# Three tiles of the pooled input move to the context's tiles, with a new order of copies, masks and norms around them

## The chip, the cores and the metric

One NeuronCore of a Trainium2 chip runs the whole program in one launch. The metric is the device time of an execution in microseconds (us), from its start to its end; less is better. TensorE (PE) multiplies matrices, VectorE (DVE), ScalarE (ACT) and GpSimd (POOL) work on elements, SyncE (SP) issues all DMAs from one queue, in order. Each engine runs its instructions strictly in the order in which the program put them there, and waits at the first whose inputs or buffers are not ready.

## The reference

One layer of a hybrid trunk, fp32, 1024 latent tokens (a grid of 16 x 64) and 256 context tokens, width 1024:

```python
h = rms_norm(x) * (1 + scale) + shift                 # modulated, as is the context
q, k, v, ab, z, u, zp = split(h @ w_in)               # one projection, q..z of 8 heads x 128
o = gated_delta_rule(conv(q), conv(k), conv(v), ...)  # 8 heads, both directions, chunks; decay masked to a triangle
y1 = norm(o) * silu(z)
y2 = (box_mean(u) - u) @ pool_w * scale * silu(zp)    # 4 groups, windows 2, 4, 8, 16
out = rms_norm(x + gate * (concat(y1, y2) @ w_out))
```

The context's tokens go through the same projection (only k and v of them are needed) and give the state with which the latent scans begin.

## The kernel before

**Tiles.** The input projection is done in tiles of 128 output columns. Every fp32 operand is split into a high part, rounded to fp32r, and a low part (the rest), and a product takes three passes (high by high, low input by high weights, high input by low weights). A tile over the 1024 latent tokens (letters `h` for a head's v, k, z or q, `z` for a gate of the pooling, `u` for a pooled input) is 48 matmuls of 128x512, in two halves; a tile over the context (`c`) is 24 matmuls of 128x256; `a` makes the decays. A tile's weights come by one DMA of 512 KB (`wraw`, or `kT` for some early ones); ScalarE makes `whi`, GpSimd `wlo`.

**Order.** `SEQ` and what follows it give the order of the tiles, and `main()` walks through it. All other work is in threads (`x_sums`, `inputs`, `thread_a` and so on), which a planner, class `Flow`, weaves in between by the costs in `Engine.cost`. It runs while the program is built, so on the chip the order on each engine is fixed. In the code all engine calls go through one helper line, L364, and all DMAs through L382; operations are therefore told apart by the names of their tiles.

**The front.** After the modulation, TensorE runs `c` tiles. Each is evacuated by ScalarE (`u<-mm`, `kT<-mm` or `vT<-mm`) and then convolved on VectorE: four `scalar_tensor_tensor` of 128x256, a tanh on ScalarE and a fifth `scalar_tensor_tensor`. Beside them the latent input x, eight tiles of 128 tokens (four in each half: `B`, `ks`, `qd` are their buffers), is normalised: a sum of squares on ScalarE (`vn`), the root on GpSimd (`rstd`, two operations), the product on VectorE. `x_half` then transposes it on TensorE in 16 pieces of 128x512 (`pp<-ident,B` and so on), ScalarE modulates each into `tmp`, `W`, `XT` or `Y` in turn, `x_split` has VectorE make `hnhi` (CAST) and VectorE or GpSimd `hnlo`. Only when all 16 are split (flag `hn`) can a tile over the latent tokens start. The first such tiles are two `z` tiles, whose evacuation needs a tanh on ScalarE (`tmp<-mm`) and one operation on VectorE (`ks<-tmp,mm`).

**The heads.** Thirty-two `h` tiles with `z` tiles among them, and for every head in turn `stage_a` to the scan. `stage_d` loads a head's decays (`D<-gscr`) and has GpSimd add a triangular mask to them (`D<-D,mask`, 128x512, four for every head and four for each of two groups of context heads), before ScalarE takes the exponential.

**The tail.** After the last tile of `main()` the heads' buffers are released and `out_main` begins: `u_tiles` runs the eight `u` tiles on TensorE (evacuated by ScalarE into three buffers `ups`, in turn), `mix_all` makes the box means on VectorE (tiles `ws`, `rp`; at the end of each `dhi` on ScalarE and `dlo` on VectorE), `pool_out` multiplies each group by its weights `pw` and evacuates with a VectorE operation (`zp<-pp,psc,zp`) and a DMA to `yscr`. The output projection takes the first three token tiles together, 288 matmuls of 128x512: first those of the heads' eight k tiles (flag `heads`), then those of the pooled eight. `second_half` loads the weights for the latter once the last `dlo` is there (flag `mixed`). Five more token tiles follow.

Of the kernel before, what the change touches and what calls it, by code (L numbers as in the profile page):

```python
# [8 lines left out]
FP32 = mybir.dt.float32  # L9
FP32R = mybir.dt.float32r  # L10
I32 = mybir.dt.int32
ACTF = mybir.ActivationFunctionType
# [19 lines left out]
DRAMS = ("gscr0", "gscr1", "escr", "sscr", "yscr", "zscr", "uscr", "gate", "ds", "vs")  # L32
SEQ = "cccccccccccccczccazhhhzhhhhhhhhhhhhhhhhhhhhhhhhhhhhh"
KB = 3
# [279 lines left out]
class Engine:  # L314
# [3 lines left out]
    def cost(self, op, a, k):  # L318
# [24 lines left out]
        if op == "tensor_copy":  # L343
            return 80.0 + 3.8 * n
        if op == "memset":
            return 36.0 + 0.83 * n
# [44 lines left out]
def kernel(  # L391
# [90 lines left out]
    ident = const.tile([P, P], FP32, name="ident")  # L482
    mask = [const.tile([P, P], FP32, name=f"mask{d}") for d in range(2)]
    tri = [dl_tile([P, P], "S", 2) for d in range(2)]
# [48 lines left out]
    for d in range(2):  # L533
        pool.memset(mask[d], 0.0)
        pool.memset(tri[d], 1.0)
        s = 1 if d == 0 else -1
        pool.affine_select(out=mask[d], in_=mask[d], pattern=[[s, P]], compare_op=ALU.is_ge, fill=NEG,
                           base=0, channel_multiplier=-s)
        pool.affine_select(out=tri[d], in_=tri[d], pattern=[[s, P]], compare_op=ALU.is_ge, fill=0.0,
                           base=0, channel_multiplier=-s)  # L540
# [23 lines left out]

    def norm_root(col):
        s = rstd[:, col:col + 1]
        pool.tensor_scalar(out=s, in0=s, scalar1=1.0 / D, scalar2=EPS, op0=ALU.mult, op1=ALU.add)
        power(s, 0)
# [87 lines left out]
    CH = [2 * g + i for g in GROUPS for i in range(2)]  # L656
    NZ = tiles[:tiles.index("h")].count("z")
    kinds = dict(c=iter([t * D + h * P for h in range(H) for t in (1, 2)]),
# [54 lines left out]
    def x_sums():  # L713
        for k in range(NB):
            flow.settle(landed[k])
            yield "act" if XACT & 1 else None
            norm_sum(xs[k], k)
            norm_root(k)
            yield "dve" if XACT & 2 else None
            norm_mul(xs[k], k)  # L720
            if k % 4 == 3:
                flow.flag("xs", k // 4)

# [245 lines left out]
    def stage_d(J, part):  # L969


        t = J.PT[part] = dl_tile([P, 2, 4, P], f"D{part}", 2)
        r = J.h * (NB if J.is_x else NBC)
        for d in range(2):
            rd = r + 4 * (part ^ d)
            sync.dma_start(out=t[:, d].rearrange("p b i -> p (b i)"), in_=gscr[J.is_x][d, rd:rd + 4, :].rearrange(
                "b i -> (b i)").partition_broadcast(P))
        yield
        for d in range(2):
            pool.tensor_tensor(out=t[:, d], in0=t[:, d], in1=rep(mask[d], 4), op=ALU.add)  # L980
            if d or DY < 8:
                yield
            for b in range(4):
                act.activation(out=t[:, d, b, :], in_=t[:, d, b, :], func=ACTF.Exp,
                               bias=J.col("ngc", d, 4 * (part ^ d) + b))
                if b % DY == DY - 1:
                    yield "act" if XACT & 16 else None
        flow.flag("D", J.key, part)
# [399 lines left out]
    def x_half(hf):  # L1388
        for k in range(KT):
# [9 lines left out]
            if XACT & 4:  # L1399
# [3 lines left out]
                           scale=md[:, 0, 1, k:k + 1], bias=md[:, 0, 0, k:k + 1])  # L1403
            flow.give()
            flow.flag("h32", n)
            flow.add(x_split(hf, k, h32), [("h32", n)], True)

    def x_split(hf, k, h32):
        if XACT & 8:
            yield "dve"  # L1410
        dve.tensor_copy(hn[2 * hf][:, k, :], h32)
        yield
        e = dve if k % XD == 0 else pool
        e.tensor_tensor(out=hn[2 * hf + 1][:, k, :], in0=h32, in1=hn[2 * hf][:, k, :], op=ALU.subtract)
        flow.flag("split", hf * KT + k)
# [29 lines left out]
    def z_tile(h):  # L1445
# [3 lines left out]
        flow.flag("z", h)  # L1449

    def zp_tile(t):

        yield ("hn",)
        if t > 1:
            yield ("zp", t - 2)
        zs = dl_tile([P, L], "ks", 2)
        yield from gate_tile(hnx, zs)
        sync.dma_start(out=zscr[CH[t]], in_=zs)
        flow.flag("zp", t)

# [23 lines left out]
    def thread_a():  # L1484
# [3 lines left out]
        for k in range(-2, H):  # L1488
            yield ("k", k)
            yield ("ab", k >= 0)  # L1490
            yield ("done", k - 2)
            yield from stage_a(jobs[k])

# [6 lines left out]
    def thread_s():  # L1500
        for k in range(-2, H):
# [5 lines left out]
            else:  # L1507
                yield ("ab", True)
                if NZ:
                    yield ("zp", NZ - 1)  # L1510
                yield from stage_k(jobs[k])
# [73 lines left out]
    def main():  # L1585
        kinds = dict(c=ctx, a=iter([ab_tile()]), u=iter([u_early(n) for n in range(UP)]),
                     z=iter([(zp_tile if i < NZ else zp_late)(i) for i in range(ZP)]),
# [241 lines left out]
    def out_main():  # L1829
# [139 lines left out]
        def second_half():  # L1969
            yield ("mixed",)  # L1970
            pl_p.release()
            pools["c"] = Pool(flow, tc.alloc_tile_pool(name="outc", bufs=1, side="right", reuse_waits="tile"))
# [110 lines left out]
```

## Time and profile before

| | before |
|---|---|
| median of 3 runs | 1317.15 us (1315.63 to 1318.1) |
| the profiled execution | 1321.76 us |
| its span, first to last instruction | 1320.0 us |
| mean granted TensorE clock | 0.962 |
| busy: PE, DVE, ACT, POOL | 1212.5, 928.0, 570.8, 438.7 us |
| instructions of 128x512 projection matmuls | 3 x 768 |

The busy times are of the whole span; what an engine does in one stage is read from windows, and what it waited for from the timeline. A matmul's record is longer than its share of the engine, since matmuls overlap; their number in a window in which TensorE never waits gives the time of one.

### The profile page before, as it was taken

The page shows a single profiled execution, that of the slowest core. Times are in us where ns is not written, and L with a number is a line of the kernel's source. Part 1 is how long each engine was busy: PE and PEld are TensorE (multiplying, and loading weights), DVE is VectorE, ACT ScalarE, POOL GpSimd, SP SyncE. Part 2 cuts the span into 40 slices and gives each one's busy share as a digit, 9 for nine tenths or more (in the row PEclk, how much of TensorE's full clock was granted, in tenths as well). Part 3 has the DMA queues.
Part 4 walks back from the last instruction along what each step waited for, and adds up shares of the span by engine and source line. Part 5 has one row for each costly group of instructions (what it writes and reads, how often), then busy time and mean ns, then how long its engine had stood idle before and what let it go on. Part 6 is the DMA issues. An engine that isn't in the chain of part 4 may idle for free.

```text
span 1320.0 us, 26398 instructions
## 1 busy us (share of the span) xinstructions
PE 1212.5 (92%) x10631; PEld 977.8 (74%) x10631; DVE 928.0 (70%) x1883; ACT 570.8 (43%) x1498; POOL 438.7 (33%) x451
## 2 busy tenths in 40 slices
PE   8876699899899999999999989999999999799997
PEld 2666577677777877788778768778788777688887
DVE  4799989868886787877776867878433999724212
ACT  3466437444436547455474464643613123322110
POOL 2477433230421423314132233141215454402330
PEclk9788899899999999989999999999999899899999
DMA  9533344223121213212221131212313135565230
GB/s 329 188 99 93 86 140 125 74 57 90 37 49 48 78 42 100 58 46 80 49 83 44 41 100 41 69 63 43 103 60 109 48 104 185 199 206 157 83 112 32
DMA packets 157384, 123.73 MB, mean 94 GB/s; under 512 B 47106, under 2 KB 135115, under 8 KB 157261
## 3 DMA queue, kind: packets, MB, share of 16 engines
q1 hardware_dynamic: 157261, 122.04, 30.6%
q8 instruction: 83, 1.36, 0.4%
q14 instruction: 40, 0.33, 0.1%
HBM read 101.43 MB, written 20.60 MB: 92 GB/s over the span
## 4 chain that ended last, share of the span: by engine, by line
PE 40%; DVE 14%; ACT 6%; DMA 2%; issue 2%; POOL 2%; DVEq 0%; SPq 0%; POOLq 0%; ACTq 0%
PE mm L364 24%; PE sc L364 5%; PE o L364 4%; DVE kT L364 4%; PE pp L364 3%; PE pa L364 3%; DVE t L364 3%; DVE ws L364 3%; ACT junk L364 2%; ACT ks L364 1%; DMA D<-gscr 1%; DVE dlo L364 1%; DVE rp L364 1%; POOL wlo L364 1%; DVE zp L364 1%
## 5 line engine op out<-in xcount | busy, mean ns | idle before, releaser
L364 PE MATMUL mm<-hnhi,whi 128*128 128x512 f32 x768 | 321.0, 418 | 0.9 <-ACT whi L364 0.9
L364 PE MATMUL mm<-hnhi,wlo 128*128 128x512 f32 x768 | 316.7, 412 | 2.0 <-POOL wlo L364 2.0
L364 PE MATMUL mm<-hnlo,whi 128*128 128x512 f32 x768 | 316.9, 413 | 0.0
L364 POOL TENSOR_TENSOR wlo<-wraw,whi 128x512 fp32r<-128x512 f32 x110 | 158.0, 1442 | 337.3 <-ACT whi L364 330.5
L364 PEld LDWEIGHTS mm<-hnhi,whi 128*128 128x128 f32 x768 | 147.7, 192 | 26.8 <-issue 1.7
L364 PEld LDWEIGHTS mm<-hnhi,wlo 128*128 128x128 f32 x768 | 146.9, 191 | 26.0 <-POOL wlo L364 2.5
L364 PEld LDWEIGHTS mm<-hnlo,whi 128*128 128x128 f32 x768 | 147.6, 192 | 22.9
L364 DVE SCALAR_TENSOR_TENSOR kT<-u,cw,kT 128x512 f32<-128x512 f32 (+1 forms) x96 | 94.8, 994 | 5.3 <-ACT kT L364 1.8
L364 POOL TENSOR_TENSOR D<-D,mask 128x512 f32<-128x512 f32 x40 | 58.9, 1478 | 92.3 <-DMA D<-gscr 76.8
L364 ACT ACTIVATE y<-sc 128x256 f32<-128x256 f32 (+1 forms) x65 | 24.9, 383 | 131.3 <-PE sc L364 125.3
L364 ACT ACTIVATE u<-mm 128x512 f32<-128x512 f32 (+1 forms) x64 | 34.8, 543 | 88.3 <-PE mm L364 88.1
L364 DVE SCALAR_TENSOR_TENSOR t<-t,laneN 128x1 f32<-128x1 f32 (+4 forms) x150 | 68.0, 453 | 6.8 <-DMA laneN<-ds 2.8
L364 ACT ACTIVATE whi<-wraw 128x512 fp32r<-128x512 f32 x110 | 67.5, 633 | 1.8 <-DMA wraw<-in_w_in_dram 1.5
L364 DVE SCALAR_TENSOR_TENSOR vT<-u,cw,vT 128x512 f32<-128x512 f32 (+1 forms) x80 | 67.2, 843 | 1.5
L364 DVE TENSOR_TENSOR pw<-mm,zp 128x512 f32<-128x512 f32 (+1 forms) x12 | 8.0, 669 | 83.9 <-PE mm L364 83.9
L364 ACT ACTIVATE D<-D,ngc 128x128 f32<-128x128 f32 x160 | 53.1, 403 | 30.7 <-POOL D L364 30.7
L364 DVE SCALAR_TENSOR_TENSOR qT<-u,cw,qT 128x512 f32<-128x512 f32 (+1 forms) x80 | 63.0, 788 | 2.9 <-ACT qT L364 1.2
L364 DVE SCALAR_TENSOR_TENSOR S<-S,egl,sc 128x128 f32<-128x128 f32 x112 | 33.7, 343 | 33.4 <-PE sc L364 30.4
L364 DVE SCALAR_TENSOR_TENSOR r<-sc,neg,vn 128x128 f32<-128x128 f32 x128 | 38.7, 345 | 23.0 <-PE sc L364 22.9
L364 PEld LDWEIGHTS sc<-S,kT 128*128 128x128 f32 x256 | 36.9, 192 | 15.6 <-issue 9.1
L364 PE MATMUL mm<-D,whi 128*128 128x256 f32 x128 | 41.2, 322 | 7.3 <-DVE ks L364 4.5
L364 PE MATMUL sc<-S,kT 128*128 128x128 f32 x256 | 40.7, 282 | 7.2 <-DVE S L364 6.7
(409 smaller groups left out, 2785.5 us busy)
## 6 DMA issues: line engine op xcount, KB each, us to landing
wraw<-in_w_in_dram SPq DMA_DIRECT2D x55, 512.0 KB, 3.8
D<-gscr SPq DMA_DIRECT2D x40, 256.0 KB, 4.1
qd<-escr SPq DMA_DIRECT2D x16, 512.0 KB
kT<-in_w_in_dram SPq DMA_DIRECT2D x9, 512.0 KB, 4.0
whnhi<-in_w_mod_dram SPq DMA_DIRECT2D x8, 512.0 KB, 3.5
whnlo<-in_w_mod_dram SPq DMA_DIRECT2D x8, 512.0 KB, 9.5
D<-in_w_mod_dram SPq DMA_DIRECT2D x8, 512.0 KB, 4.9
yscr<-zs SPq DMA_DIRECT2D x8, 512.0 KB, 2.8
```

What stands on the lines that cost most here:

```text
L364: return f(*a, **k)
```

## The change

- `SEQ`: instead of 14 `c`, `z`, 2 `c`, `a`, `z` ahead of the first head there are 11 `c`, `u`, 2 `c`, `u`, 2 `c`, `u`, `a`, `c`, `z`. The number of tiles is the same; one `z` more comes behind the last head's tiles (six instead of five).
- The three early `u` tiles are evacuated by two ScalarE copies each into a `ks` buffer and stored to `uscr`; after the heads they are read back into `ups`. Five `u` tiles stay in the tail.
- `x_half`: ScalarE makes `hnhi` right after the modulated piece, and `x_split` is left with the subtraction for `hnlo`. `thread_a` also waits until the first half's pieces are made.
- `stage_d`: one `affine_select` in place of the addition of a mask; the two mask tiles and their making are gone.
- `x_sums`: four sums of squares, one root for four columns, four products, instead of one after the other.
- `second_half` also waits for the last group's pooling weights.

```diff
-SEQ = "cccccccccccccczccazhhhzhhhhhhhhhhhhhhhhhhhhhhhhhhhhh"
+SEQ = "cccccccccccuccuccuaczhhhzhhhhhhhhhhhhhhhhhhhhhhhhhhhhh"
...
-    def norm_root(col):
-        s = rstd[:, col:col + 1]
+    def norm_root(col, n=1):
+        s = rstd[:, col:col + n]
...
     def x_sums():
-        for k in range(NB):
-            flow.settle(landed[k])
-            yield "act" if XACT & 1 else None
-            norm_sum(xs[k], k)
-            norm_root(k)
-            yield "dve" if XACT & 2 else None
-            norm_mul(xs[k], k)
-            if k % 4 == 3:
-                flow.flag("xs", k // 4)
+        for hf in range(2):
+            ks = range(4 * hf, 4 * hf + 4)
+            for k in ks:
+                flow.settle(landed[k])
+                yield "act"
+                norm_sum(xs[k], k)
+            yield
+            norm_root(4 * hf, 4)
+            for k in ks:
+                yield "dve"
+                norm_mul(xs[k], k)
+            flow.flag("xs", hf)
...
         for d in range(2):
-            pool.tensor_tensor(out=t[:, d], in0=t[:, d], in1=rep(mask[d], 4), op=ALU.add)
+            s = 1 - 2 * d
+            pool.affine_select(out=t[:, d], in_=t[:, d], pattern=[[0, 4], [s, P]], compare_op=ALU.is_ge, fill=NEG,
+                               base=0, channel_multiplier=-s)
...
             flow.give()
+            act.activation(out=hn[2 * hf][:, k, :], in_=h32, func=ACTF.Copy)
             flow.flag("h32", n)
             flow.add(x_split(hf, k, h32), [("h32", n)], True)
+        flow.flag("xt", hf)
 
     def x_split(hf, k, h32):
-        if XACT & 8:
-            yield "dve"
-        dve.tensor_copy(hn[2 * hf][:, k, :], h32)
-        yield
+        yield "pool" if k % XD else "dve"
         e = dve if k % XD == 0 else pool
...
+    def ahead(dst, tile):
+
+        i = aheads[0]
+        aheads[0] += 1
+        yield ("hn",)
+        if i > 1:
+            yield ("ahead", i - 2)
+        s = dl_tile([P, L], "ks", 2)
+        yield from tile(s)
+        sync.dma_start(out=dst, in_=s)
+        flow.flag("ahead", i)
...
+    def u_tile(n):
+        def tile(s):
+            def evac(ps, t0):
+                act.activation(out=s[:, t0:t0 + 512], in_=ps, func=ACTF.Copy)
+
+            yield from gemm_tile(hnx, L, evac)
+
+        yield from ahead(uscr[n], tile)
...
-                if NZ:
-                    yield ("zp", NZ - 1)
+                if NZ + NUA:
+                    yield ("ahead", NZ + NUA - 1)
...
         def second_half():
             yield ("mixed",)
+            yield ("pw", GROUPS[-1])
```

**Where instructions move.** On TensorE, ahead of the first tile that reads `hn`, before: the transposes of x's second half (from `ks` and `qd`) stand among the matmuls of `c` tiles (`mm<-D` and `mm<-zs`).

```order
L364 MATMUL mm<-D_230,wlo 128x256
L364 MATMUL pp<-ident,ks 128x128 x2
L364 MATMUL pp<-ident,qd 128x128 x2
L364 MATMUL mm<-D_230,whi 128x256
L364 MATMUL mm<-zs,whi 128x256
L364 MATMUL mm<-D_230,wlo 128x256
L364 MATMUL mm<-D_229,whi 128x256
```

The same place of the changed kernel, from the last matmul of the eleventh `c` tile to the first of the first `u` tile, with the middle left out:

```order
L366 MATMUL mm<-D_220,wlo 128x256
L366 MATMUL pp<-ident,B 128x128 x8
L366 MATMUL pp<-ident,ks 128x128 x2
L366 MATMUL pp<-ident,qd 128x128 x2
L366 MATMUL pa<-kT 128x128 x4
...
L366 MATMUL pp<-ident,ks 128x128 x2
L366 MATMUL pp<-ident,qd 128x128 x2
L366 MATMUL pa<-ident,vT 128x128 x4
L366 MATMUL mm<-hnhi_223,whi 128x512
L366 MATMUL mm<-hnlo_224,whi 128x512
```

All eight transposes of the second half, and two of the first, now stand between the eleventh `c` tile and the first `u` tile with no tile's matmuls among them.

On ScalarE, the last pieces of x before the change:

```order
L364 ACTIVATE tmp<-pp,md 128x512
L364 ACTIVATE W<-pp,md 128x512
L364 ACTIVATE u<-mm 128x256
L364 ACTIVATE qT<-mm,cw 128x256
L364 ACTIVATE D_983<-D_983,ngc_238 128x128 x4
L364 ACTIVATE whi<-kT 128x512
L364 ACTIVATE XT<-pp,md 128x512
L364 ACTIVATE whi<-kT 128x512
L364 ACTIVATE Y<-pp,md 128x512
```

and now:

```order
L366 ACTIVATE tmp<-pp,md 128x512
L366 ACTIVATE hnhi_225<-tmp 128x512
L366 ACTIVATE W<-pp,md 128x512
L366 ACTIVATE hnhi_225<-W 128x512
L366 ACTIVATE XT<-pp,md 128x512
L366 ACTIVATE hnhi_225<-XT 128x512
L366 ACTIVATE t_1162<-B,half_of 32x128 x4
L366 ACTIVATE t_1162<-bt,half_of 128x128
L366 ACTIVATE D_1167<-D_1167,ngc_228 128x128 x2
L366 ACTIVATE Y<-pp,md 128x512
L366 ACTIVATE hnhi_225<-Y 128x512
```

Pieces and their copies stand in pairs, and the evacuations of `c` tiles that stood between them are ahead of them.

On SyncE's queue, the change from the heads to the tail, before:

```order
L382 DMA zscr<-u 128x1024
L382 DMA yscr<-zs 128x1024
L382 DMA pwr<-in_pool_w_dram 128x2x256
L382 DMA zp<-zscr 128x1024 x2
L382 DMA wraw<-in_w_in_dram 128x8x128 x4
```

and now (`zscr<-u` stores the last `z` tile):

```order
L384 DMA yscr<-zs 128x1024
L384 DMA zscr<-u 128x1024
L384 DMA ups_11395<-uscr 128x16x64
L384 DMA ups_11396<-uscr 128x16x64
L384 DMA ups_11397<-uscr 128x16x64
L384 DMA pwr<-in_pool_w_dram 128x2x256
L384 DMA zp<-zscr 128x1024 x2
```

The three loads of `ups` stand behind the store of the last `z` tile, which waits for that tile's last VectorE operation.

## Rows read from the trace of the kernel before

**Rows 1.** Windows: start:end length, busy us (x) of PE, PEld, DVE, ACT, POOL, granted clock, DMA.

```profile
46.00:134.50 88.50, 62.81 (x409) 58.12 (x408) 83.32 (x141) 53.12 (x122) 59.69 (x77) 0.85 0.32 90
134.50:193.20 58.70, 48.59 (x590) 36.70 (x591) 50.80 (x97) 23.35 (x63) 23.20 (x24) 0.91 0.36 101
...
260.00:1005.00 745.00, 708.58 (x7577) 582.23 (x7575) 538.41 (x1285) 368.46 (x1066) 210.96 (x213) 0.98 0.22 62
1016.80:1138.50 121.70, 113.28 (x480) 91.55 (x479) 116.85 (x110) 32.52 (x45) 59.42 (x34) 0.97 0.33 107
1160.00:1200.00 40.00, 40.00 (x178) 33.02 (x177) 9.95 (x12) 9.64 (x15) 9.52 (x8) 1.00 0.50 164
```

**Rows 2.** VectorE's operations by form, 46 to 134.5 us: busy us, mean ns, idle before.

```profile
L364 DVE SCALAR_TENSOR_TENSOR vT<-u,cw,vT 128x256 f32<-128x256 f32 x16 | 15.3, 956 | 0.4
L364 DVE SCALAR_TENSOR_TENSOR kT<-u,cw,kT 128x256 f32<-128x256 f32 x23 | 15.2, 659 | 2.3 <-ACT kT L364 1.8
L364 DVE CAST hnhi<-XT 128x512 fp32r<-128x512 f32 x4 | 6.2, 1554 | 0.0
L364 DVE CAST hnhi<-tmp 128x512 fp32r<-128x512 f32 x4 | 4.0, 1003 | 0.2 <-ACT tmp L364 0.2
...
L364 DVE CAST hnhi<-W 128x512 fp32r<-128x512 f32 x4 | 2.7, 683 | 0.0
...
L364 DVE CAST hnhi<-Y 128x512 fp32r<-128x512 f32 x4 | 2.6, 638 | 0.0
```

**Rows 3.** Timeline of VectorE, 680 to 701 us: start, length, operation.

```profile
683.68 11.27 DVE L364 SCALAR_TENSOR_TENSOR kT<-u,cw,kT 128x512 f32<-128x512 f32 x8
...
699.86 1.29 DVE L364 SCALAR_TENSOR_TENSOR kT<-u,kT 128x512 f32<-128x512 f32 x2
```

**Rows 4.** Timeline of GpSimd, same stretch.

```profile
685.31 1.28 POOL L364 TENSOR_TENSOR wlo<-wraw,whi 128x512 fp32r<-128x512 f32 x1 [2.59 <-ACT whi L364]
686.53 1.75 POOL L364 TENSOR_TENSOR D<-D,mask 128x512 f32<-128x512 f32 x1
```

**Rows 5.** GpSimd's operations by form, 46 to 134.5 us.

```profile
L364 POOL TENSOR_TENSOR D<-D,mask 128x512 f32<-128x512 f32 x4 | 5.9, 1482 | 0.0
...
L364 POOL TENSOR_TENSOR rstd<-rstd,expo 128x1 f32<-128x1 f32 x8 | 5.5, 684 | 0.7
```

**Rows 6.** ScalarE's operations by form, 46 to 134.5 us.

```profile
L364 ACT ACTIVATE W<-pp,md 128x512 f32<-128x512 f32 x4 | 3.1, 779 | 1.9 <-PE pp L364 1.9
```

**Rows 7.** Timeline of TensorE at the first matmul that reads hn.

```profile
134.51 0.50 PE L364 MATMUL mm<-hnhi,whi 128*128 128x512 f32 x1 [0.87 <-ACT whi L364]
```

**Rows 8.** TensorE's waits, 134 to 194 us: tile, releaser, total us, times, longest.

```profile
PE mm L364 <- DVE ks L364: 4.5, 1, 4.5
```

**Rows 9.** GpSimd's affine_select on tile t: count, ns min/median/max, first and last start.

```profile
L364 POOL TENSOR_SCALAR_AFFINE_SELECT t<-t x10: 510/510/705, 145.6 to 900.4; 128x256 f32<-128x256 f32 x10
```

**Rows 10.** TensorE's waits, 200 to 960 us.

```profile
PE pa L364 <- DVE kT L364: 12.4, 7, 3.6
```

**Rows 11.** Timeline of VectorE, the end of the heads and the pooling.

```profile
1005.31 0.69 DVE L364 SCALAR_TENSOR_TENSOR u<-tmp,mm 128x512 f32<-128x512 f32 x1 [4.44 <-ACT tmp L364]
...
1016.77 1.58 DVE L364 TENSOR_TENSOR ws<-ups 128x1120 f32<-128x1120 f32 x1 [1.36 <-ACT ups L364]
...
1136.11 0.74 DVE L364 SCALAR_TENSOR_TENSOR zp<-pp,psc,zp 128x512 f32<-128x512 f32 x1
1137.32 1.23 DVE L364 TENSOR_TENSOR dlo<-ws,dhi 128x1024 fp32r<-128x1024 f32 x1 [0.47 <-ACT dhi L364]
```

**Rows 12.** Timeline of SyncE's queue: a load of y pieces is issued.

```profile
1100.88 0.38 SPq L382 DMA_DIRECT2D wraw<-yscr  x1
```

**Rows 13.** Timeline of ScalarE: the first operation that reads what was loaded.

```profile
1106.67 1.06 ACT L364 ACTIVATE yhi<-wraw 128x1024 fp32r<-128x1024 f32 x1 [3.51 <-DMA wraw<-yscr]
```

**Rows 14.** GpSimd's operations by form, 1016.8 to 1138.5 us.

```profile
L364 POOL TENSOR_TENSOR wlo<-wraw,whi 128x512 fp32r<-128x512 f32 x12 | 24.4, 2046 | 36.3 <-ACT whi L364 36.3
```

**Rows 15.** Timeline of TensorE at the last pooled group.

```profile
1144.92 0.80 PE L364 MATMUL pp<-dhi,pw 128*128 128x512 f32 x1 [7.06 <-ACT pw L364]
```

More of the change, by code (lines that the diff above doesn't have):

```diff
@@ L344, in cost @@
             return 80.0 + 3.8 * n
+        if op == "affine_select":
+            return 80.0 + 1.7 * n
         if op == "memset":
@@ L482 @@
     ident = const.tile([P, P], FP32, name="ident")
-    mask = [const.tile([P, P], FP32, name=f"mask{d}") for d in range(2)]
     tri = [dl_tile([P, P], "S", 2) for d in range(2)]
@@ L533 @@
     for d in range(2):
-        pool.memset(mask[d], 0.0)
         pool.memset(tri[d], 1.0)
         s = 1 if d == 0 else -1
-        pool.affine_select(out=mask[d], in_=mask[d], pattern=[[s, P]], compare_op=ALU.is_ge, fill=NEG,
-                           base=0, channel_multiplier=-s)
         pool.affine_select(out=tri[d], in_=tri[d], pattern=[[s, P]], compare_op=ALU.is_ge, fill=0.0,
@@ L656 @@
     CH = [2 * g + i for g in GROUPS for i in range(2)]
-    NZ = tiles[:tiles.index("h")].count("z")
+    NZ, NUA = [tiles[:tiles.index("h")].count(c) for c in "zu"]
     kinds = dict(c=iter([t * D + h * P for h in range(H) for t in (1, 2)]),
@@ L1449, in z_tile @@
         flow.flag("z", h)
-    def zp_tile(t):
[L1453 to L1459, printed above, removed]
+    def ahead(dst, tile):
[8 more added lines that the diff above has]
+        flow.flag("ahead", i)
+    aheads = [0]
+    def zp_tile(t):
+        yield from ahead(zscr[CH[t]], lambda s: gate_tile(hnx, s))
+    def u_tile(n):
[4 more added lines that the diff above has]
+        yield from ahead(uscr[n], tile)
     def zp_late(t):
@@ L1491, in thread_a @@
             yield ("done", k - 2)
+            yield ("xt", 0)
             yield from stage_a(jobs[k])
@@ L1585, in main @@
     def main():
-        kinds = dict(c=ctx, a=iter([ab_tile()]), u=iter([u_early(n) for n in range(UP)]),
+        kinds = dict(c=ctx, a=iter([ab_tile()]), u=iter([(u_tile if n < NUA else u_early)(n) for n in range(UP)]),
                      z=iter([(zp_tile if i < NZ else zp_late)(i) for i in range(ZP)]),
```

## Prediction

> **What bounds the kernel now.** I read the windows by stage first, then for each stage the engine that never rests. TensorE is nearly full through the heads (708.6 of 745 us from 260 to 1005) and full in the output projection; what it loses, it loses at both ends [rows 1]. From 46 to 134.5 us it works 62.8 of 88.5 us, and VectorE 83.3: VectorE is the bound, and `hn`, the point at which the first tile over the latent tokens can start, came at 134.51 [rows 1, 7]. From there to 193.2, where the first head's tile starts, TensorE rests another 58.7 - 48.6 = 10.1 us, 4.5 of them because a `z` tile's evacuation stood in VectorE's queue [rows 1, 8]; the clock of 0.91 means that some 18% of the stretch ran at the lower level, which cost about 5 us. In the tail VectorE is the bound again: the pooling runs on it from 1016.77 to 1138.5 and fills 116.9 of 121.7 us, while TensorE has 113.3 us of records there and then a wait of 7 us for the last group's weights [rows 1, 11, 15]. So the tail is as long as VectorE's chain, not as TensorE's work. A tile of 48 matmuls costs 48 x 40 / 178 = 10.8 us at full clock, from the window without waits [rows 1].
>
> **VectorE is slowed by GpSimd.** The eight steps of a k convolution took 11.27 us, 1.41 each, while GpSimd ran additions and subtractions of 1.28 and 1.75 us; two steps of the same size just behind them took 0.65 each [rows 3, 4]. In the front the 256-wide steps took 0.66 and 0.96 us on average, about twice what half of 0.65 would be, and one kind of CAST took 0.64 and another 1.55 [rows 2].
>
> **Step 1, when `hn` comes.** The 16 casts leave VectorE: 6.2 + 4.0 + 2.7 + 2.6 = 15.5 us [rows 2]. GpSimd loses two-input work there: six of eight roots (0.68 each), the splits of the three `c` tiles that now come later (six of about 1.4), a part of the masks (5.9 in all) [rows 5], together some 15 of its 59.7 us. VectorE's 39 convolution steps of these two kinds hold about 17 us above half of 0.65 each, so I credit 15/59.7 of that, 4 us. Against it, VectorE's order now has two more convolutions and a few small operations of the context's stage ahead of the last split, about 4 us. That gives 134.5 - 15.5 - 4 + 4 = 119. ScalarE now has 16 copies more, at about the 0.78 of a piece or less [rows 6], and in the order the last eight pieces stand as pairs with nothing between them: they cannot start before VectorE has normalised x's second half, behind its convolutions. I take 121. The bounds are 110 (every us that GpSimd gives back is one of VectorE's) and 131 (the copies, some 10 us, come wholly behind VectorE).
>
> **Step 2, from `hn` to the first head.** Now four tiles (43.2 us), five `c` tiles (24 matmuls of half the width, 2.7 each, 13.5), the decays (32 matmuls, 7.2) and the context's own stage. That stage is what remains of the old stretch: 58.7 - 10.1 waits - 5 for the clock - 21.6 - 5.4 - 7.2 = 9.4. The `u` tiles are evacuated by ScalarE alone, so the 4.5 us wait on VectorE should go; of the old 15 us of waits and low clock I keep 6. Sum 79, so the first head starts at 200 instead of 193.2: **+7**. TensorE does two tiles (21.6 us) more by then, so 15 of them are hidden; the pauses from 46 on had room for 36.
>
> **Step 3, heads.** The order keeps four tiles to a head, so their length stays except for waits. One mask addition in each head falls into the k convolution, for whose end TensorE waited seven times, 12.4 us in all [rows 4, 10]. The trace has no select of 128x512; one of half the size took 0.51 [rows 9], so between 0.51 and 1.02 against 1.28 to 1.75. If it slows VectorE for as long as it lasts, a head gains some 0.4 us, if not at all up to 1.7; **-4**, bounds 0 and -12. The Trainium skill ("SBUF — State Buffer", SBUF: two separate sides) says that GpSimd and VectorE share a port pair that is locked for a whole instruction, by any GpSimd operation that reads SBUF against a VectorE operation with two SBUF inputs. The convolution's 1.41 against 0.65 agrees with it; by that rule the select still locks VectorE out while it runs, and this step would be nearer to -3.
>
> **Step 4, one `z` tile more behind the heads: +10.8.** It stands ahead of everything in the tail on every queue that matters: VectorE's pooling comes behind its gate, and SyncE's loads of `ups` behind its store.
>
> **Step 5, start of the pooling.** Before, it began 10.8 us after the last gate (1006.0 to 1016.77), the time of a `u` tile [rows 11]. Now it needs a read-back. The nearest row is the load of `yscr`, 5.8 us from issue to its first use [rows 12, 13]; with 5.5 this is **-5.3** (bounds -4 and -7.5).
>
> **Step 6, the pooling itself.** The same operations on VectorE. Under them stood 12 weight splits of 2.05 us on GpSimd [rows 14]; with five `u` tiles left it is eight. **-5**, bounds 0 and -8.2. The 33 us of TensorE's work that leave the tail give nothing: TensorE has five tiles (54), twelve of sixteen pool products (16) and 66 output matmuls (15) to do before the last group, 85 us, against VectorE's 5.5 + 117 + 6. It will rest some 43 us there.
>
> **Step 7, after the last `dlo`.** Before, the last group's first product came 6.4 us after `dlo`, 8.1 us after the evacuation that frees the way for its weights [rows 11, 15]. Now that evacuation stands behind the last `dlo`, but fewer loads stand ahead of the weights. From that product to the end of the first three token tiles the order has 246 matmuls instead of 237. **+2**, bounds 0 and +5. The 120 us behind them are unchanged.
>
> **Sum.** 7 - 4 + 10.8 - 5.3 - 5 + 2 = +5.5 us. The profiled execution took 1321.76 us (span 1320.0), 4.6 above the median of the runs; so 1327.3 for one like it, and 1317.15 + 5.5 = **1322.7** for the median. Costed at nothing: the mask tiles, made at the program's start while the modulation's weights are loading, at most four operations of 0.51 us on GpSimd if that cover were gone [rows 9]; the three stores of 512 KB to `uscr`, on DMA engines that are busy 0.36 of that stretch [rows 1]; the wait added to `thread_a`, behind which the context's first stage is queued, whose matmuls stand among the last transposes and have four tiles beside them (uncovered it would be part of rival B); and the wait in `second_half`, behind which only loads stand that are needed some 30 us later.
>
> **Rivals.**
> A, faster: VectorE gets the whole of what GpSimd gives back, and `hn` comes at 110. Then everything behind it is 11 us earlier: 1311 to 1312. For it: the convolution row shows nearly one us lost for each us of GpSimd. Against it: the last eight pairs on ScalarE have to follow the normalisation. It decides at an `hn` of about 115.5, where the sum is nil.
> B, a new wait: the pairs on ScalarE become the bound, `hn` at 131, hardly earlier than before. 5.5 + 10 = 15.5, so 1333. For it: no tile's matmuls stand beside the last transposes, so nothing covers them.
> C, the tail follows TensorE's work: the three tiles taken out (32.4 us) come off its end. With steps 2 to 4 that is 7 - 4 + 10.8 - 32.4, about 1299. Against it: VectorE's 117 us in 122.
> D, the select or the read-back does not give what I credit: steps 3, 5 and 6 at their poor bounds make 5.5 + 4 + 1.3 + 5, 1333; it shares its place with B.
>
> **How the numbers follow.** What a measurement can tell from no change is about 0.2%, 2.6 us. The forecast (1317 to 1329) has 0.5, A (1307 to 1316) 0.25, B with D (1329 to 1337) 0.19, C 0.06. Slower is all of B and D and three quarters of the forecast: 0.57. No change is the forecast's lower end and a little of A: 0.14. Faster is the rest: 0.29. The range goes from 1306 to 1335, which leaves out C and the ends of A and B.
>
> **What would show it.** The first matmul that reads `hn` at 121, the first head's tile at 200; the last gate about 14 us later than before; the first `ws<-ups` 5.5 us behind it; the last `dlo` 117 us after that; and TensorE resting some 40 us in the tail. The sum is wrong if `hn` comes before 115, or if VectorE is not busy through the pooling.

## The result, and the profile after

The changed kernel took 1329.76 us (median of 4 runs, 1327.1 to 1332.19) against 1317.27 us for the kernel before on the same chip (4 runs, 1315.63 to 1318.1): a ratio of 1.0096 [1.0071, 1.012], some 12.5 us slower. Slower was the forecast's sign; its 1322.7 was 7 us short, inside the range.

The two profiled executions stand closer together than the medians: their spans are 1320.0 and 1325.4 us, since the one before lies above the median of its kernel and the one after (1327.1 us) is the fastest of its own. The steps below are read from that pair and add up to +5.4 us; the other 7 us of the medians' difference have no place in it.

Windows of the changed kernel (columns as in [rows 1]): the front up to `hn`, from `hn` into the first head's tile, the heads with the last `z` tile, the pooling.

```profile
46.00:124.80 78.80, 52.27 (x335) 47.31 (x336) 70.49 (x124) 56.23 (x124) 45.25 (x56) 0.82 0.29 82
124.80:221.90 97.10, 89.82 (x879) 70.30 (x878) 52.51 (x105) 39.75 (x98) 29.44 (x38) 0.93 0.31 84
230.10:1016.60 786.50, 755.67 (x8108) 617.05 (x8107) 584.28 (x1373) 402.03 (x1147) 219.00 (x237) 0.99 0.25 71
1024.00:1141.00 117.00, 80.32 (x311) 62.43 (x310) 112.84 (x112) 28.12 (x38) 56.34 (x30) 0.84 0.38 121
```

`hn` came 9.7 us earlier than in [rows 7], but TensorE's rest ahead of it did not shrink: 88.5 - 62.8 = 25.7 us in [rows 1], 78.8 - 52.3 = 26.5 here. Behind it comes a stretch of 97 us in place of 59. In the tail TensorE rests 37 us while VectorE is full.

TensorE's timeline ahead of `hn` and behind it (last bracket: idle time before, and its releaser):

```profile
107.93 1.11 PE L366 MATMUL pp<-ident,B 128*128 128x128 f32 x4 [9.10 <-ACT W L366]
...
118.21 0.44 PE L366 MATMUL pp<-ident,ks 128*128 128x128 f32 x2 [0.93 <-ACT Y L366]
...
124.80 0.78 PE L366 MATMUL mm<-hnhi,whi 128*128 128x512 f32 x1
```

The longest wait, 9.10 us, is for ScalarE's piece `W`. ScalarE was not full then: `W` stands behind a tanh of a `c` tile, and that waited for VectorE's convolution:

```profile
105.62 0.42 ACT L366 ACTIVATE u<-kT 128x256 f32<-128x256 f32 x1 [3.85 <-DVE kT L366]
```

After it the last transposes come at ScalarE's pace, most of them waiting some 0.9 us for a pair of piece and copy, with no tile's matmuls beside them.

TensorE's operations by form, 124.8 to 221.9 us: busy us and mean ns, idle before.

```profile
L366 PE MATMUL mm<-hnhi,whi 128*128 128x512 f32 x69 | 29.5, 428 | 0.7 <-ACT whi L366 0.7
...
L366 PE MATMUL mm<-zs,whi 128*128 128x256 f32 x40 | 11.5, 287 | 0.0
```

In [rows 1]'s second window these were 33 and 16: the two tiles over the latent tokens and the three `c` tiles that are new in this stretch are all here. ScalarE's first evacuation of the first head's v tile, before and after:

```profile
199.10 0.68 ACT L364 ACTIVATE vT<-mm,cw 128x512 f32<-128x512 f32 x1
```

```profile
230.12 0.75 ACT L366 ACTIVATE vT<-mm,cw 128x512 f32<-128x512 f32 x1
```

This first evacuation is the milestone that I use below for the end of the front; it moved by 31.0 us. The prediction's milestone, the start of the first head's tile, moved by 25.3 us, from 193.2 to 218.5. The other 5.7 us lie in the first half of that tile, before and after:

```profile
193.20:199.10 5.90, 5.90 (x28) 4.89 (x27) 5.86 (x18) 2.21 (x4) 4.27 (x7) 1.00 0.60 191
```

```profile
218.50:230.10 11.60, 9.13 (x39) 7.18 (x38) 11.24 (x32) 6.40 (x20) 5.21 (x4) 0.88 0.27 93
```

A part of the context's stage now stands among its matmuls, with a rest of 2.5 us.

VectorE's timeline at the end of the heads and of the pooling, answering to [rows 11]:

```profile
1016.61 0.69 DVE L366 SCALAR_TENSOR_TENSOR u<-tmp,mm 128x512 f32<-128x512 f32 x1 [4.75 <-ACT tmp L366]
...
1023.98 1.33 DVE L366 TENSOR_TENSOR ws<-ups 128x1120 f32<-128x1120 f32 x1 [6.11 <-DMA ups<-uscr]
...
1138.55 0.74 DVE L366 SCALAR_TENSOR_TENSOR zp<-pp,psc,zp 128x512 f32<-128x512 f32 x1
1139.81 1.23 DVE L366 TENSOR_TENSOR dlo<-ws,dhi 128x1024 fp32r<-128x1024 f32 x1 [0.52 <-ACT dhi L366]
```

The last gate is 11.3 us later; behind it the three loads queue behind the gate's store, as SyncE's queue shows:

```profile
1017.32 0.32 SPq L384 DMA_DIRECT2D zscr<-u  x1
1017.73 5.99 SPq L384 DMA_DIRECT2D ups<-uscr  x3
```

TensorE's waits, 200 to 960 us and then 1010 to 1150 us (total us, times, longest):

```profile
PE sc L366 <- DVE r L366: 9.9, 10, 1.7
PE sc L366 <- DVE S L366: 8.8, 11, 1.6
```

```profile
PE mm L366 <- ACT ups L366: 13.1, 1, 13.1
```

The wait of [rows 10], 12.4 us for the k convolutions, is gone (0.4 us are left); shorter waits of the scan stand in its place. In the tail TensorE waits 13.1 us after the first `u` tile of the five, until that tile has been evacuated into a buffer `ups` which the pooling was using.

| step | forecast | profiled pair | how read |
|---|---|---|---|
| 1 `hn` | 134.5 to 121 | 134.5 to 124.8 | first matmul of `hn` |
| 2 front | +7 | +31.0 | 199.10 to 230.12 (head's tile: +25.3) |
| 3 heads, without 4 | -4 | -30.5 | 806.2 to 786.5 less 10.8 |
| 4 one `z` more | +10.8 | +10.8 (10.3 in e4) | |
| 5 gate to pooling | -5.3 | -4.1 | 11.46 to 7.37 |
| 6 pooling | -5 | -4.7 | 121.8 to 117.1 |
| 7 after `dlo` | +2 | +2.9 | 181.45 to 184.36 |
| sum | +5.5 | +5.4 | |

So the sum of the pair is nearly the forecast's, out of two terms that are each some 25 us off, with opposite signs. Counted from the start of the head's tile, as the forecast was, they are +25.3 and -24.8: 18 and 21 us off.

### The profile page after: what moved, and what is told of

Same layout as the page of the kernel before. It is cut to its first block, busy times and chain, and to the rows that moved or that the text cites. A ratio compares the mean times of both kernels' runs of the same rounds, so it can differ in the third digit from the quotient of the medians.

```text
span 1325.4 us, 26426 instructions
## 1 busy us (share of the span) xinstructions
PE 1205.4 (91%) x10631; PEld 966.1 (73%) x10631; DVE 907.0 (68%) x1867; ACT 583.1 (44%) x1514; POOL 410.3 (31%) x435
## 4 chain that ended last, share of the span: by engine, by line
PE 49%; DVE 29%; ACT 8%; DMA 6%; issue 4%; POOL 3%; SPq 1%; DVEq 0%; POOLq 0%; ACTq 0%
PE mm L366 29%; DVE kT L366 6%; PE sc L366 5%; PE pp L366 5%; PE o L366 5%; DVE t L366 4%; PE pa L366 4%; DVE vT L366 3%; DVE ws L366 3%; DMA wraw<-yscr 2%; ACT ks L366 1%; DVE B L366 1%; DVE dlo L366 1%; DVE D L366 1%; ACT u L366 1%
## 5 line engine op out<-in xcount | busy, mean ns | idle before, releaser
L366 PE MATMUL mm<-hnhi,whi 128*128 128x512 f32 x768 | 319.9, 417 | 13.9 <-ACT ups L366 13.1
L366 PE MATMUL mm<-hnhi,wlo 128*128 128x512 f32 x768 | 321.0, 418 | 0.7 <-POOL wlo L366 0.7
L366 DVE SCALAR_TENSOR_TENSOR kT<-u,cw,kT 128x512 f32<-128x512 f32 (+1 forms) x96 | 103.4, 1081 | 6.5 <-ACT u L366 1.9
L366 DVE SCALAR_TENSOR_TENSOR t<-t,laneN 128x1 f32<-128x1 f32 (+4 forms) x150 | 61.9, 412 | 13.5 <-POOL t L366 7.4
L366 DVE SCALAR_TENSOR_TENSOR qT<-u,cw,qT 128x512 f32<-128x512 f32 (+1 forms) x80 | 58.5, 738 | 3.6 <-ACT qT L366 1.7
L366 PEld LDWEIGHTS sc<-r,B 128*128 128x128 f32 x256 | 36.0, 190 | 20.1 <-DVE r L366 9.0
L366 PE MATMUL sc<-r,B 128*128 128x128 f32 x256 | 41.1, 283 | 10.2 <-DVE r L366 9.9
L366 ACT ACTIVATE ks<-pp,sm 128x128 f32<-128x128 f32 x160 | 43.5, 390 | 15.3 <-PE pp L366 12.4
L366 POOL TENSOR_TENSOR ylo<-wraw,yhi 128x1024 fp32r<-128x1024 f32 (+2 forms) x9 | 20.2, 2244 | 93.0 <-ACT yhi L366 93.0
```

The costliest lines, as they stand in the source:

```text
L366: return f(*a, **k)
```

## The experiments

All kernels compute the full reference. Times are medians, each beside runs of the kernel before on the same chip; since the latter had medians of 1316.06, 1318.87 and 1317.33 us in the three groups of runs, differences across groups are good to some 2 us. Theory: the loss is the tiles' new order in the front, the gain in the heads is the select. Rivals: the new plan's order gives the gain; or the tail or the copies take it back.

**e1, the select alone.** The kernel before with the change's select, woven by the planner at the select's cost:

```diff
-            pool.tensor_tensor(out=t[:, d], in0=t[:, d], in1=rep(mask[d], 4), op=ALU.add)
+            s = 1 - 2 * d
+            pool.affine_select(out=t[:, d], in_=t[:, d], pattern=[[0, 4], [s, P]], compare_op=ALU.is_ge, fill=NEG,
+                               base=0, channel_multiplier=-s)
```

> The kernel before with the masks' addition replaced by the select and nothing else. In the changed kernel the heads took 796 us for the same tiles instead of 811.5, and the waits of TensorE for the k convolution went from 12.4 to 0.4 us. Theory 1: that is the select's doing, since it runs 0.68 us instead of 1.48 on GpSimd and blocks VectorE less; then this kernel takes 1301 to 1307 us, and the wait for kT is gone here too. Theory 2: it comes from the new order of the tiles ahead of the heads, and the select gives at most 4 us: 1313 to 1318.

Measured: 1308.52 us, 0.9907 [0.9871, 0.9942]. Faster, but less than theory 1 said, and with two of the six runs at 1298 and 1299 us and four at 1308 to 1309. TensorE's wait for the k convolutions is 5.0 us, not gone.

**e2, the changed kernel with the mask's addition back.** The reverse edit.

> The changed kernel with the masks' addition put back and nothing else. Theory 1 (the select shortens the heads): 11 to 16 us over the changed kernel, 1340 to 1346, with TensorE's wait for kT back at 10 us or more. Theory 2 (the order of the tiles does): 1329 to 1334.

Measured: 1356.69 us, 1.028 [1.0243, 1.0318]: 27 us above the changed kernel, more than either theory said, so the select is worth more here than the whole change costs. The planner's order differs from the changed kernel's as well; e9 takes that apart. The heads of e2 with the one `z` tile more, from the first v to the last gate:

```profile
232.80:1046.80 814.00, 766.97 (x8107) 629.54 (x8107) 585.26 (x1374) 399.92 (x1147) 233.18 (x237) 0.97 0.24 69
```

These are 814.0 us where the changed kernel takes 786.5. Without the 10.8 of the `z` tile they are 803, only 3 us under the 806 of before: the other 27.5 of the 30.5 us in step 3 came with the select.

**e3, the changed kernel with the old order of tiles** (select, copies and grouped norms stay):

```diff
-SEQ = "cccccccccccuccuccuaczhhhzhhhhhhhhhhhhhhhhhhhhhhhhhhhhh"
+SEQ = "cccccccccccccczccazhhhzhhhhhhhhhhhhhhhhhhhhhhhhhhhhh"
```

> The changed kernel with the old SEQ, so no u tile ahead of the heads and no z tile more behind them; copies, select and norms stay. Theory 1: the moved tiles are what costs, since the front hides only a part of them and the tail cannot use the room; the rest of the change gives 10 us in the front and 11 to 15 in the heads: 1291 to 1298. Rival: the early u tiles are hidden and the loss is elsewhere (copies on ScalarE, the new wait): 1320 to 1330.

Measured: 1294.33 us, 0.9819 [0.9793, 0.9844]. Taking back the order of tiles gains 35 us.

**e4, one `z` tile put behind the heads into the tail** (the planner's `POST`: what `main()` leaves to the tail):

```diff
-POST = ""
+POST = "z"
```

> The changed kernel with its last z tile run as the first tile of the tail (POST = z) instead of the last one behind the heads, the same work. Theory 1: the tail is as long as VectorE's pooling, and TensorE rests some 40 us in it, so the tile is hidden there except for its two gates and two weight splits, 3 to 4 us: 7 us less than the changed kernel, about 1322. Rival: TensorE's work sets the tail: no change, 1328 to 1331.

Measured: 1319.43 us, 1.0016 [0.9995, 1.0037], 10.3 us under the changed kernel: nearly the whole of a tile's 10.8. VectorE's start and end of the pooling in e4:

```profile
1016.76 2.12 DVE L366 TENSOR_TENSOR ws<-ups 128x1120 f32<-128x1120 f32 x1 [0.82 <-DMA ups<-uscr]
```

```profile
1131.70 1.22 DVE L366 TENSOR_TENSOR dlo<-ws,dhi 128x1024 fp32r<-128x1024 f32 x1 [0.53 <-ACT dhi L366]
```

The tail takes a whole tile more on TensorE and its chain from `ws` to the end of `dlo` is 116.2 us, not longer than 117.1. VectorE sets it; this speaks against rival C.

**e5, the select at the old order.** e1's edit, but planned at the addition's cost, so that the orders on TensorE, VectorE, ScalarE and SyncE stay those of the kernel before (the mask tiles are still made, at the start):

```diff
+        if op == "affine_select" and n == 512:
+            return 148.0 + 2.1 * n
```

> The kernel before with the select, but planned as if it still were the addition: on TensorE, VectorE, ScalarE and SyncE every instruction stands where it stood before, and on GpSimd only the 40 operations differ. Before with the select and its own plan took 1308.5 us against 1316.1. Theory 1 (the shorter operation gives the gain): 1301 to 1309. Theory 2 (the plan's new order gives it): 1313 to 1318.

Measured: 1285.93 us (1285.15 to 1288.37), 0.9756 [0.973, 0.9783]. This is the fastest kernel of the study: 33 us under before, twice what theory 1 said, and 44 under the change. Since only the operation differs, the two traces can be laid side by side. One head, from the start of its k convolution to the start of the next head's, in the kernel before (the first window is the head, the second 5 us in it):

```profile
683.68:772.91 89.23, 83.92 (x893) 69.36 (x892) 68.74 (x159) 46.02 (x135) 26.37 (x26) 0.96 0.22 62
```

```profile
700.00:705.00 5.00, 4.40 (x20) 4.15 (x21) 3.05 (x6) 0.82 (x2) 0.00 (x0) 0.66 0.00 0
```

```profile
700.60 2.06 PE L364 MATMUL pa<-kT 128*128 128x128 f32 x8 [2.66 <-DVE kT L364]
```

A second wait of this head, and the 5 us behind it:

```profile
730.99 0.91 PE L364 MATMUL sc<-y,ks 128*128 128x128 f32 x4 [1.77 <-ACT y L364]
```

```profile
731.00:736.00 5.00, 5.00 (x23) 4.43 (x24) 4.72 (x12) 1.80 (x5) 2.44 (x3) 0.66 0.07 12
```

The same head with the select, on VectorE, in a window, and 5 us at the place of the first wait:

```profile
662.14 8.50 DVE L366 SCALAR_TENSOR_TENSOR kT<-u,cw,kT 128x512 f32<-128x512 f32 x8
```

```profile
662.14:746.05 83.91, 81.13 (x893) 66.48 (x892) 64.87 (x159) 46.20 (x135) 23.43 (x26) 1.00 0.24 65
...
675.00:680.00 5.00, 4.95 (x37) 4.43 (x36) 4.18 (x8) 1.45 (x4) 0.33 (x3) 1.00 0.00 0
```

The same 893 matmuls and 159 VectorE operations take 83.91 us instead of 89.23. The convolution falls from the 11.27 us of [rows 3] to 8.50, TensorE's wait of 2.66 us is gone, and so is what followed it: the granted clock of 0.66 in the 5 us from 700, with two thirds of them at the lower of the two levels, 1.2 GHz, which is some 1.7 us of work lost (5 x 0.34). The second wait is shorter in e5 (1.27 for 1.77 us), and its 1.7 us of low clock is gone too: the head's granted clock is 1.00. So of this head's 5.3 us 2.5 are rest and 2.8 TensorE's busy time, from the low clock at both places.

**e6, the addition at the new order.** The kernel before, its addition woven as if it cost what the select does; the order is that of e1:

```diff
-            pool.tensor_tensor(out=t[:, d], in0=t[:, d], in1=rep(mask[d], 4), op=ALU.add)
+            pool.mask_add(out=t[:, d], in0=t[:, d], in1=rep(mask[d], 4), op=ALU.add)
...
-        f = getattr(self.real, op)
+        f = getattr(self.real, "tensor_tensor" if op == "mask_add" else op)
```

> The other way round: the addition of the mask stays, but it is planned at the select's cost, so that the order is that of the run with the select alone. Theory 1 (shorter operation): 1314 to 1322, and TensorE's wait for kT is back. Theory 2 (order): 1301 to 1310.

Measured: 1322.79 us, 1.0023 [1.0004, 1.0043]. The new order is no gain: +4 us with the addition, and +22 with the select (e1 against e5; 13 by the fastest run of each). In both orders the select in place of the addition pays, 33 us at the old one, some 15 at the new. But TensorE's wait for the k convolutions is not back, as theory 1 had it: 5.2 us here, 5.0 in e1. And these are no shorter with the select at this order. In e6 and in e1, 200 to 960 us:

```profile
L366 DVE SCALAR_TENSOR_TENSOR kT<-u,cw,kT 128x512 f32<-128x512 f32 x64 | 75.2, 1180 | 3.8 <-ACT u L366 1.3
```

```profile
L366 DVE SCALAR_TENSOR_TENSOR kT<-u,cw,kT 128x512 f32<-128x512 f32 x64 | 79.2, 1243 | 3.8 <-ACT u L366 1.3
```

So here the gain came another way than through the k convolution. From the first v to the last gate TensorE rests 50.3 us in e6 (809.6 - 759.3) and 38.5 in e1 (789.4 - 750.9); the difference is spread over many shorter waits, and which operations the select shortened for them was not taken apart.

**e7, e3 with one `z` tile in the tail** (`POST = "z"`, as in e4).

> The changed kernel with the old SEQ (1294.3 us) and one of the five z tiles that stand behind the heads moved into the tail, ahead of the eight u tiles. Theory 1: TensorE has only some 15 us of room in the old tail, of which the tile's two gates and splits on VectorE take a part: 2 to 6 us less, 1288 to 1292. Rival: with eight u tiles TensorE's work already sets the tail, so the pooling only begins 10.8 us after the heads as it did: 1293 to 1298.

Measured: 1312.03 us, 0.9947 [0.9929, 0.9965], 18 us worse than e3; my theory fell here. TensorE in e7, while the last head's scan runs, in the timeline and in two windows of 6 us:

```profile
981.16 2.29 PE L366 MATMUL pp<-ident,ks 128*128 128x128 f32 x8 [5.57 <-ACT ks L366]
```

```profile
972.00:978.00 6.00, 2.55 (x16) 2.01 (x16) 0.72 (x3) 2.60 (x13) 0.00 (x0) 1.00 0.01 1
978.00:984.00 6.00, 2.84 (x10) 2.21 (x11) 1.44 (x3) 3.95 (x14) 4.62 (x14) 0.53 0.00 0
```

With four `z` tiles behind the last head instead of five, the end of the last scan has no matmuls beside it, and the tail's `z` stands ahead of the first `u` tile for which the pooling waits: that began at 1006.8, after 988.5 in e3. In e4 five tiles were left there, and the pooling began with what had been stored early.

**e8b, the old tiles with three `c` moved behind the first `z`** (no early `u`; a first order for this test, e8, with `z`, 4 `c`, `a`, `c`, `z` behind the eleven, deadlocks and has no time):

```diff
-SEQ = "cccccccccccuccuccuaczhhhzhhhhhhhhhhhhhhhhhhhhhhhhhhhhh"
+SEQ = "ccccccccccczcczcccahhhzhhhhhhhhhhhhhhhhhhhhhhhhhhhhh"
```

> The changed kernel with eleven c tiles first and then z, two c, z, three c, a: the front begins as in the changed kernel, but the two old z tiles stand where the early u tiles stood, and all eight u tiles are in the tail. Theory 1 (the three early u tiles and the z tile behind the heads cost, the start with eleven c tiles does not): 1284 to 1298, as with the old SEQ or a little less. Rival (the front loses because the last transposes stand without a tile beside them): 1305 to 1320.

Measured: 1313.91 us, 0.9976 [0.9959, 0.9993]. Its front, in windows up to `hn` and from there to the first evacuation of v:

```profile
46.00:126.50 80.50, 55.42 (x336) 50.02 (x336) 71.48 (x127) 56.55 (x125) 45.15 (x56) 0.78 0.28 80
126.50:208.80 82.30, 72.19 (x786) 55.37 (x785) 50.99 (x108) 34.31 (x83) 27.52 (x39) 0.87 0.35 97
```

`hn` comes 13.7 us earlier than in e3 (140.2), the first head's v 11.2 later (197.6 there): with no `u` tile at all, an early `hn` paid for by `c` tiles behind it is lost again, at a clock of 0.87. In all it is 20 us slower than e3. Why the heads then take 792.6 us, after e3's 779.4, stays open.

**e9, the changed kernel with the select planned at the addition's cost** (e5's two lines). TensorE's order is that of e2.

> The changed kernel with the select planned at the addition's cost, so that TensorE has the order of the run with the mask added back (1356.7 us). Theory 1 (the shorter operation is worth some 30 us at a given order, here too): 1323 to 1330. Theory 2 (in the changed kernel, as in the one before, planning at the select's cost loses 22 us as well): 1305 to 1312.

Measured: 1331.37 us, 1.0101 [1.0069, 1.0133]: like the changed kernel, and 25 us under e2, which is the select's worth at a fixed order on TensorE, VectorE, ScalarE and SyncE.

**e10, e3 with e5's two lines**: e5 with copies on ScalarE and grouped norms.

> Old SEQ, copies on ScalarE, norms and select, planned at the addition's cost; beside the run with the select in the old order (1285.9 us) it shows the copies and norms alone. Theory 1 (VectorE bounds the front, so the 16 casts taken from it bring hn forward): 1272 to 1282, hn before 128 us. Rival (with 14 c tiles first the copies make ScalarE late, as hn at 140 us under the old SEQ says): 1288 to 1298, hn near 140.

Measured: 1293.66 us (1286.49 to 1294.74), 0.9808 [0.9773, 0.9844]. Against e5's 0.9756 [0.973, 0.9783] that is some 8 us slower by the medians, but the intervals touch. TensorE's longest waits up to `hn` in e10, and in e5:

```profile
PE pp L366 <- ACT W L366: 13.1, 2, 12.2
```

```profile
PE pp L366 <- ACT tmp L366: 3.8, 2, 2.8
```

In e10 a transpose waits 12.2 us for ScalarE's `W`, and `hn` comes at 140.1 instead of 131.7: with the old order of tiles the copies and norms, with the planner's order that comes with them, do not bring `hn` forward, they delay it. It is not that the copies fill ScalarE. `W` stands behind the last `c` tiles' tanhs, which wait for VectorE's convolutions, as in the changed kernel:

```profile
122.81 0.42 ACT L366 ACTIVATE u<-qT 128x256 f32<-128x256 f32 x1 [3.41 <-DVE qT L366]
```

e3 against e1 shows the same delay at the select's cost: `hn` at 140.2 for 129.7.

**e11, the tiles alone**: the changed kernel with the addition, VectorE's casts and the single norms back, and without the new wait in `thread_a`. What is left of the change is `SEQ`, the early `u` tiles and the wait in `second_half`.

```diff
-            act.activation(out=hn[2 * hf][:, k, :], in_=h32, func=ACTF.Copy)
...
+        dve.tensor_copy(hn[2 * hf][:, k, :], h32)
...
-            yield ("xt", 0)
```

> The tiles' new order alone: three early u tiles, one z tile more behind the heads, with the mask's addition, the casts on VectorE and the single norms of the kernel before. By my prediction's terms for the tiles (7 + 10.8 - 5.3 - 5 + 2) it takes 9 to 10 us more than before, 1324 to 1330. If the front hides nothing of the two tiles more (21.6 instead of 7), which the runs with the old SEQ suggest, 1336 to 1346.

Measured: 1359.27 us, 1.0321 [1.0289, 1.0353]: +42 us, more than either case said. e2, which has the copies, the norms and the wait besides, is at 1.028 [1.0243, 1.0318], and the two intervals overlap: at the new order they are worth some 5 us at most by these medians. Its windows, as above:

```profile
46.00:124.90 78.90, 53.84 (x332) 48.84 (x330) 74.31 (x124) 45.84 (x105) 52.97 (x66) 0.80 0.27 75
124.90:226.00 101.10, 92.97 (x882) 73.31 (x881) 58.91 (x120) 40.23 (x99) 34.26 (x40) 0.91 0.31 86
235.00:1047.30 812.30, 765.59 (x8107) 627.57 (x8106) 584.53 (x1373) 399.92 (x1147) 234.36 (x237) 0.98 0.24 69
```

`hn` stands at 124.9 here too, with the casts on VectorE. The first v is evacuated at 235.0 (+35.9); heads (with one `z` tile more, 10.8 us), read-back, pooling and end give +6.1, -3.8, -4.8 and +2.4, in sum 35.8, the difference of the spans (1355.8 to 1320.0).

## Why the sign was right and two terms were not

**Step 1: right within 4 us, for a wrong reason.** I took `hn` from 134.5 to 121 by what leaves VectorE. e11 gives none of that back to VectorE and has `hn` at 124.9, as the whole change has it at 124.8; e10 has all of it, with the old tiles, and `hn` is later than in e5. `hn` moved because three `c` tiles, with their matmuls, evacuations and convolutions, stand behind it instead of ahead of it; e8b, with these three moved and no early `u`, has it at 126.5. Rival B's part, pairs on ScalarE with nothing beside them, is there in the waits of 0.9 us. The larger waits, 9.1 here and 12.2 in e10, are for ScalarE's order: pieces that stand behind tanhs of `c` tiles, and so behind VectorE's convolutions. What VectorE is spared and what these waits cost about cancel: e11, without the copies, has `hn` as early. A, with `hn` at 110, did not happen. (The steps of 0.96 us that I called about twice the half of 0.65 are three times that; the 17 us that I drew from both kinds stand within 1 us.)

**Step 2: the term that failed most, +7 for +25 by its own milestone and +31 by the first v.** I forecast the first head's tile at 200, 79 us behind an `hn` of 121. `hn` came 3.8 us later than that. The window of 97.1 us ends 13 matmuls of 128x512 into the head's tile (205 of these, four tiles being 192), some 3 us, so the stretch took 94. The missing 15 are sizes of its terms: by the subtraction that I had used (205 x 0.225, 120 x 0.112, 32 x 0.225 us, some 67 of the 89.8 busy us), 7 us are a clock of 0.93 and 16 the context's stage, for which I had 9; rest and low clock together are 14, for which I had 6. For the 5.7 us more inside the head's tile I had no term.

The reason that I gave for the +7 was wrong as well: that 15 of the 21.6 us of the two tiles are hidden, since "the pauses from 46 on had room for 36". They had, and they still have: 26.5 us up to `hn` and 97.1 - 89.8 = 7.3 behind it, 33.8 in all. A `u` tile reads `hn`, as every tile over the latent tokens does, so it cannot stand in a pause that ends with `hn`; it can only fill pauses behind it, of which there were 10.1 us [rows 1]. e3 and e11 confirm the place: without the tiles 1294.33, with them alone +42. But not all of the 35 us between e3 and the changed kernel are the `u` tiles': e8b, which has none of them early, loses 20 by moving three `c` tiles behind `hn`.

**Step 3: the mechanism in part, six to seven times too small, -4 for -25 to -30.** I bounded it by TensorE's listed waits for the k convolution, 12.4 us, and took a third. The select's length was not what I had wrong: 0.85 us on average lies in my 0.51 to 1.02. In 200 to 960 us of the kernel before the addition and the convolution it slows stand as

```profile
L364 POOL TENSOR_TENSOR D<-D,mask 128x512 f32<-128x512 f32 x32 | 47.3, 1484 | 92.3 <-DMA D<-gscr 76.8 <-PE sc L364 10.2 <-DVE qd L364 5.3
```

```profile
L364 DVE SCALAR_TENSOR_TENSOR kT<-u,cw,kT 128x512 f32<-128x512 f32 x64 | 74.4, 1172 | 2.6
```

and in e5, at the same order, as

```profile
L366 POOL TENSOR_SCALAR_AFFINE_SELECT D<-D 128x512 f32<-128x512 f32 x32 | 26.9, 845 | 91.4 <-DMA D<-gscr 81.2 <-PE sc L366 10.2
```

```profile
L366 DVE SCALAR_TENSOR_TENSOR kT<-u,cw,kT 128x512 f32<-128x512 f32 x64 | 62.1, 980 | 2.6
```

So the convolutions give 12.3 us, some 1.5 to a head, near the upper end of what I had for one. Two things were missing. First, GpSimd's work under one convolution shrank by more than the operation did. In the kernel before it goes on behind the two operations of [rows 4] as

```profile
690.31 1.28 POOL L364 TENSOR_TENSOR wlo<-wraw,whi 128x512 fp32r<-128x512 f32 x1 [2.03 <-ACT whi L364]
691.55 5.65 POOL L364 TENSOR_TENSOR qd<-qd,qT 128x1024 f32<-128x1024 f32 x2
```

and in e5, under the convolution from 662.14 to 670.64, it is

```profile
663.77 1.28 POOL L366 TENSOR_TENSOR wlo<-wraw,whi 128x512 fp32r<-128x512 f32 x1 [3.53 <-ACT whi L366]
665.00 1.09 POOL L366 TENSOR_SCALAR_AFFINE_SELECT D<-D 128x512 f32<-128x512 f32 x1
668.78 1.31 POOL L366 TENSOR_TENSOR wlo<-wraw,whi 128x512 fp32r<-128x512 f32 x1 [2.70 <-ACT whi L366]
670.05 5.21 POOL L366 TENSOR_TENSOR qd<-qd,qT 128x1024 f32<-128x1024 f32 x2
```

`qd<-qd,qT` starts 7.9 us behind the convolution's start in both. Before, 3.4 us of the convolution were left then, to run beside it; in e5 0.6. So 0.66 us less of GpSimd (1.75 to 1.09) came to 2.77 us less of convolution; that the one is the cause of the other is read from these rows and was not tried by itself. Second, my upper bound of 12 counted only the listed rest for one releaser. The heads before and in e5:

```profile
199.10:1005.30 806.20, 763.45 (x8172) 624.66 (x8171) 593.38 (x1389) 406.04 (x1172) 231.41 (x229) 0.97 0.23 65
```

```profile
191.60:969.20 777.60, 751.46 (x8172) 615.23 (x8171) 567.87 (x1391) 406.22 (x1172) 209.81 (x229) 0.99 0.24 68
```

Of the 28.6 us 16.6 are rest, of which the waits for the k convolution gave 8.8 (12.4 to 3.6) and others the remainder, and 12.0 are TensorE's busy time, with a clock of 0.99 for 0.97. Another 7.5 us come in e5 ahead of the first v (199.1 to 191.6), where step 1 had 4 for all the work that leaves GpSimd. e9 against e2 shows the same, 25 us with shorter convolutions (947 ns a step for 1108). But the convolution is not the only way. In the changed kernel itself its steps are no shorter than before (1225 ns for 1172), nor are they in e1 against e6, and the heads gain all the same; by which operations, no run shows.

The Trainium skill ("SBUF — State Buffer", SBUF: two separate sides) has GpSimd and VectorE exclude each other for a whole instruction, where GpSimd reads SBUF and the VectorE operation has two SBUF inputs. The rows fit that for the select as well. Eight steps at the 0.65 us of [rows 3] would be 5.2: before, 6.07 us were lost under 1.28 + 1.75 + 1.28 + 3.4 = 7.7 of GpSimd work, in e5 3.30 under 1.28 + 1.09 + 1.31 + 0.6 = 4.3; the ratio is the same, 0.77 to 0.79, with the select counted as blocking, and without it more would be lost (3.30) than lay beside it (3.19). But the -3 us that I drew from the rule for this step were wrong, since the size hung on what else the convolution then no longer ran beside.

**Steps 4 to 7: right within 1.2 us each.** The `z` tile cost 10.8, and e4 got 10.3 back by moving one; the pooling began 6.7 us behind the gate's end where I had 5.5 after the nearest row [rows 12, 13]; the pooling shrank by 4.7 with the four weight splits that left it (eight stand there now, 16.9 us, instead of the twelve of [rows 14]); TensorE rests 37 us there where I had 43. The 32 us of TensorE's work taken out of the tail gave nothing, as I had said against rival C.

**Rivals.** The measured 1329.76 lies just above the forecast's own case (1317 to 1329), and the number of B and D (1333) is nearer than 1322.7, but their mechanisms did not happen: `hn` came at 124.8, and the select gave far more than I credited. No case that I had written has both large terms; the sum came out by their cancelling, and that the time lay in the range is luck. Of the signs that I had named, only the first head's tile at 200 was plainly missed.

## What to carry to other kernels

Before work is moved into an engine's idle time, ask whether its inputs exist while the engine is idle: a pause that ends with the arrival of an input has no room for work that reads it. Price a removed wait by a whole period of the loop, rest and low clock together (28.6 us here for 8.8 of listed waits), and look at what the shortened operation no longer runs beside. When a planner orders by costs, a new cost changes the order too: test the operation at the old order first; here that was worth 33 us, and at the order of the planner's own choice 22 of them were lost by the medians.

## What was not expected of the hardware

- A select of 128x512 on GpSimd takes 0.63 to 1.10 us (40 in the changed kernel, median 0.68), the addition of a mask of the same size 1.27 to 2.22 (median 1.37). The row of half the size [rows 9] had suggested up to 1.02.
- TensorE waits of 2.66 and of 1.77 us were each followed by 5 us at a granted clock of 0.66, some 1.7 us of work lost each time; behind one of 1.27 us in e5 the clock stayed at 1.00.
- Three loads of 512 KB read back from `uscr` kept VectorE waiting 6.11 us; their issue follows that of the last gate's store in SyncE's queue.
